# Gate and up with 512 weight columns moving, whole-chunk splits, and two Strassen groups per SwiGLU

## The chip, the cores and the metric

The kernel runs on one core of a Trainium2 chip. The metric is the device time of one execution in microseconds. Three runs of the kernel before gave a median of 753.91 us (753.84 to 754.42). One further execution was recorded by the hardware profiler, and the views quoted below come from that one. The engines are PE (matmul), DVE (vector), ACT (scalar), POOL (GpSimd) and SP, which issues most of the loads.

## The reference, cut to what matters

One decoder layer, x of (1, 256, 1024) in float32, every sublayer between two RMS norms:

```
h = h + 0.5 * rmsnorm(swiglu(rmsnorm(h, g1), w_gate, w_up, w_down), p1)      # FFN1, d_ff = 2816
u = rmsnorm(h, g2)
z, xbc, dt, q, k, v, gates = split(u @ w_in)                                   # the mix stage
h = h + rmsnorm((sig0 * ssd(z, xbc, dt) + sig1 * diff_attn(q, k, v)) @ w_out, p2)
h = h + 0.5 * rmsnorm(swiglu(rmsnorm(h, g3), w_gate, w_up, w_down), p3)      # FFN2
swiglu(x, wg, wu, wd) = (silu(x @ wg) * (x @ wu)) @ wd
```

## The kernel before, in words

There are 256 tokens, two blocks of 128. Every float32 product is made of three products of fp32r parts: an operand is split into hi, an ACT cast (line 167 for weights, line 191 for tokens), and lo, a DVE subtraction (lines 168 and 192), and PE adds hi·hi, lo·hi and hi·lo in PSUM.

Weights come as chunks of 1 MB (128 partitions by 2048 elements), loaded by SP into three raw tiles (`raw`). `split_steps` splits a chunk in two halves of 128x1024, each with its cast and its subtraction into `whi` and `wlo`. `take` hands out the next chunk and first splits on to `AHEAD` = 3 chunks.

The stages follow one another: FFN1 (first products `pn_f`, gate and up `pg_f` and `pup_f`, down `acc_f`), the mix stage (`pn_mx` for v, `pdt` for the time steps with the small weight `wdt`, then `pbc`, `pxs`, `pz`, `pq`, `pgt`, `pws`, `pwd`, and `acc_mx` for w_out), and FFN2 built as FFN1 is.

In an FFN the first 512 of the 2816 gate and up columns go through `norm.products`: here tokens are the stationary operand and 512 weight columns move (`mm_nat`, line 231), the output is natural (a token per partition), and `back` turns it with four transposes per block. The other nine groups of 256 columns go through `mm_w` (lines 215, 216 and 218): weights are stationary, and per 128 rows a matmul of 512 (hi and lo tokens side by side) and one of 256 come out, which puts the output on PE transposed, as the down product needs it. It is evicted by an ACT copy and a DVE addition (lines 219 and 220), multiplied on DVE (line 570) and split (lines 191 and 192). The down product `mm_n` (line 441) keeps the last three chunks (`TAIL`) back, finishes block 0 and then block 1, half after half, so that block 0's norm runs while block 1 is computed.

After each sublayer `post_norm` sums squares (ACT `jp`), takes the root on POOL (`rp`) and updates `h`; then the next norm is made: `sq` on ACT, `r` on POOL, `un` on DVE, eight transposes `pu` on PE, the split into `u`. Up to the end of the first products the order on PE, ACT, DVE and SP is program order (`own_order`); elsewhere a scheduler places the instructions of those engines, with PE held to program order in some stretches. POOL makes small constants (`m3`, `after_m`, `dneg`: masks and distances) and loads gains and small weights by its own queue.

Of the kernel before, what the change touches and what calls it, by code (L numbers as in the profile page):

```python
# [24 lines left out]
P = 128  # L25
T = 256
# [7 lines left out]
K4_BUFS = 29  # L34
K3_BUFS = 3
K2_BUFS = 7
RAW_BUFS = 3
AHEAD = 3
# [5 lines left out]
SSD_US = 1.55  # L44
BREAK, STOP = object(), object()
# [3 lines left out]
def tile_hybrid_layer(ctx: ExitStack, tc: tile.TileContext, x, ffn1_pre_g, ffn1_w_gate, ffn1_w_up,  # L49
# [9 lines left out]

    def k4(shape, name, dt=F32):  # L60
        return sb.tile(shape, dt, tag="k4", name=name, bufs=K4_BUFS)

    def k3(shape, name, dt=F32):
        return sb.tile(shape, dt, tag="k3", name=name, bufs=K3_BUFS)
# [4 lines left out]
    def jk(shape, name):  # L69
        return sb.tile(shape, F32, tag="jk", name=name, bufs=2)  # L70
# [16 lines left out]
    chunks = []  # L87

    def t_chunk(w, k0, c0):
        chunks.append((w[k0:k0 + D, c0:c0 + T].rearrange("(j p) c -> p j c", p=P), [P, KD, T]))  # L90

    def s_chunk(w, k0, c0):
        chunks.append((w[k0:k0 + 512, c0:c0 + 512].rearrange("(j p) c -> p j c", p=P), [P, 4, 512]))

    def n_chunk(w, k0):
        chunks.append((w[k0:k0 + 2 * P, :].rearrange("(j p) c -> p j c", p=P), [P, 2, D]))
# [3 lines left out]

    def ffn_chunks(wg, wu, wd):
        for w in (wg, wu):
            for k0 in (0, 512):
                s_chunk(w[0], k0, 0)
        for j in range(2, FF // T):
            t_chunk(wg[0], 0, j * T)
            t_chunk(wu[0], 0, j * T)
        for j in range(FF // T):
            n_chunk(wd[0], j * T)

    ffn_chunks(ffn1_w_gate, ffn1_w_up, ffn1_w_down)
    for c in range(2):
        for k0 in (0, 512):
            s_chunk(w_in2, k0, V0 + c * 512)
# [9 lines left out]
    for c in range(4):  # L124
        for k0 in (0, 512):
            s_chunk(w_in2, k0, G0 + c * 512)
    for c in range(2):
        for k0 in range(0, 2 * D, 512):
            s_chunk(ssd_w_branch[0], k0, c * 512)
    for c in range(2):  # L130
        for k0 in (0, 512):
            s_chunk(da_w_branch[0], k0, c * 512)
    for c in range(4):
        n_chunk(w_out[0], c * 2 * P)
    ffn_chunks(ffn2_w_gate, ffn2_w_up, ffn2_w_down)

    raws, splits = [], []
    taken = [0]

    def load_to(n):  # L140
        while len(raws) < min(n, len(chunks)):
            i = len(raws)
            src, shape = chunks[i]
            r = sb.tile(shape, F32, tag="raw", name=f"raw{i}", bufs=RAW_BUFS)
            nj = shape[1] // 4 if i == 0 else shape[1] // 2 if i < 4 else shape[1]
            for j in range(0, shape[1], nj):
                nc.sync.dma_start(r[:, j:j + nj, :], src[:, j:j + nj, :])
            raws.append(r)

    def split_steps(ahead=True):  # L150


        i = len(splits)
        load_to(i + 1)
        r, shape = raws[i], chunks[i][1]
        nj = shape[1] // 2
        his, los = [], []
        splits.append((his, los))
        for q in range(2):
            hi = k4([P, nj, shape[2]], f"whi{i}{q}", F32R)  # L160
            lo = k4([P, nj, shape[2]], f"wlo{i}{q}", F32R)
            his.append(hi)
            los.append(lo)
            n = 1 if i == 0 else nj
            for j in range(0, nj, n):
                js = slice(j, j + n)
                nc.scalar.copy(hi[:, js, :], r[:, q * nj + j:q * nj + j + n, :])  # L167
                nc.vector.tensor_sub(lo[:, js, :], r[:, q * nj + j:q * nj + j + n, :], hi[:, js, :].bitcast(F32))  # L168
                yield
        raws[i] = None  # L170
        if ahead:
            load_to(i + 1 + RAW_BUFS)

    def split_to(n):

        while len(splits) < min(n, len(chunks)):
            for _ in split_steps():
                pass

    def take(ahead=AHEAD):  # L180
# [3 lines left out]
        split_to(i + ahead)  # L184
        his, los = splits[i]
        splits[i] = None
        nj = chunks[i][1][1] // 2
        return (lambda j: his[j // nj][:, j % nj, :], lambda j: los[j // nj][:, j % nj, :])
# [17 lines left out]
    def mm_w(dst, name, w, act):  # L206


        (wh, wl), (ah, _, ahl) = w, act
        for m in range(2):  # L210
            acc = pj(f"{name}{m}")
            cs = slice(m * P, (m + 1) * P)
            for j in range(KD):
                if j:
                    nc.tensor.matmul(acc[:, :T], wl(j)[:, cs], ah(j), start=False, stop=False)  # L215
                nc.tensor.matmul(acc, wh(j)[:, cs], ahl(j), start=j == 0, stop=j == KD - 1)  # L216
                if not j:
                    nc.tensor.matmul(acc[:, :T], wl(j)[:, cs], ah(j), start=False, stop=False)
            nc.scalar.copy(dst[:, m, :], acc[:, T:])  # L219
            nc.vector.tensor_tensor(dst[:, m, :], acc[:, :T], dst[:, m, :], ALU.add)  # L220

    def mm_nat(acc, w, act, k0, first, last, late):
# [7 lines left out]
        for i, ((a, b), j) in enumerate(terms):  # L230
            nc.tensor.matmul(acc, a(k0 + j), b(j), start=first and i == 0, stop=last and i == 11)  # L231
# [43 lines left out]
    load_to(RAW_BUFS)  # L275
# [917 lines left out]
```

## Time and profile before

| | us |
|---|---|
| median of three runs | 753.91 |
| span of the profiled execution | 753.1 |
| PE busy in it | 743.7 |
| DVE busy | 521.7 |
| ACT busy | 440.1 |
| POOL busy | 38.2 |
| gate and up of FFN1, from the first `pg_f` to the first `acc_f` | 34.43 to 135.99 |
| down of FFN1 | 135.99 to 196.74 |
| mix stage, from the first `pn_mx` to the first `pn_f` of FFN2 | 196.77 to 562.26 |
| gate and up of FFN2 | 585.67 to 686.88 |

The profiled execution's span is 0.8 us below the median of the runs. A row of the timeline gives the start in the span, the duration, engine, line, operation, the tile written and the tiles read. A row of groups gives, behind the shapes, the count, the busy time in us and the mean duration in ns; behind the second bar stands how long the engine was idle just before, and what released it. Rows of matmuls overlap: what counts is the time from one start to the next.

### The profile page before, as it was taken

The page shows a single profiled execution, that of the slowest core. Times are in us where ns is not written, and L with a number is a line of the kernel's source. Part 1 is how long each engine was busy: PE and PEld are TensorE (multiplying, and loading weights), DVE is VectorE, ACT ScalarE, POOL GpSimd, SP SyncE. Part 2 cuts the span into 40 slices and gives each one's busy share as a digit, 9 for nine tenths or more (in the row PEclk, how much of TensorE's full clock was granted, in tenths as well). Part 3 has the DMA queues.
Part 4 walks back from the last instruction along what each step waited for, and adds up shares of the span by engine and source line. Part 5 has one row for each costly group of instructions (what it writes and reads, how often), then busy time and mean ns, then how long its engine had stood idle before and what let it go on. Part 6 is the DMA issues. An engine that isn't in the chain of part 4 may idle for free.

```text
span 753.1 us, 11054 instructions
## 1 busy us (share of the span) xinstructions
PE 743.7 (99%) x4377; PEld 646.1 (86%) x4377; DVE 521.7 (69%) x792; ACT 440.1 (58%) x737; POOL 38.2 (5%) x72
## 2 busy tenths in 40 slices
PE   8999999999999999999999999999999999999996
PEld 6888888888889999898999788788888888888885
DVE  6686677654577978767778988695684867766612
ACT  7475566643565565858966556784463756565511
POOL 6400000000300000000000000000010000000000
PEclk9999999999999999999999999999999999999999
DMA  8685765587253556565555463467361776555701
GB/s 300 161 265 182 224 224 207 200 286 228 64 166 116 174 163 215 165 210 176 187 168 177 165 219 127 153 224 251 112 225 56 224 224 217 173 173 183 290 1 56
DMA packets 94212, 137.96 MB, mean 183 GB/s; under 512 B 2684, under 2 KB 68304, under 8 KB 94160
## 3 DMA queue, kind: packets, MB, share of 16 engines
q1 hardware_dynamic: 91488, 129.51, 52.5%
q0 software_dynamic: 2368, 7.22, 3.1%
q8 instruction: 34, 0.56, 0.3%
q10 hardware_dynamic: 304, 0.53, 0.2%
q14 instruction: 18, 0.15, 0.1%
HBM read 136.17 MB, written 1.08 MB: 182 GB/s over the span
## 4 chain that ended last, share of the span: by engine, by line
PE 96%; DVE 1%; DMA 1%; POOL 1%; ACT 1%; issue 0%; SPq 0%; DVEq 0%; POOLq 0%
PE acc_f L441 16%; PE pup_f L216 9%; PE pg_f L216 9%; PE pws L231 6%; PE pgt L231 6%; PE pn_f L231 5%; PE pg_f L215 4%; PE pup_f L215 4%; PE acc_mx L441 3%; PE pn_mx L231 3%; PE pwd L231 3%; PE pxs L204 2%; PE pxs L202 2%; PE pxs L201 2%; PE pz L204 2%; PE pz L201 2%
## 5 line engine op out<-in xcount | busy, mean ns | idle before, releaser
L168 DVE TENSOR_TENSOR wlo<-raw,whi 128x1024 fp32r<-128x1024 f32 (+1 forms) x246 | 291.6, 1214 | 56.3 <-ACT whi L167 53.6
L167 ACT CAST whi<-raw 128x1024 fp32r<-128x1024 f32 (+1 forms) x246 | 247.3, 1044 | 59.9 <-PE acc_f L441 21.8
L216 PE MATMUL pg_f<-u_f,whi 128*128 128x512 f32 x288 | 101.2, 396 | 0.0
L216 PE MATMUL pup_f<-u_f,whi 128*128 128x512 f32 x288 | 101.1, 396 | 0.0
L215 PE MATMUL pg_f<-u_f,wlo 128*128 128x256 f32 x252 | 70.5, 280 | 0.0
L215 PE MATMUL pup_f<-u_f,wlo 128*128 128x256 f32 x252 | 70.3, 279 | 0.0
L216 PEld LDWEIGHTS pg_f<-u_f,whi 128*128 128x128 f32 x288 | 52.9, 188 | 9.7
L216 PEld LDWEIGHTS pup_f<-u_f,whi 128*128 128x128 f32 x288 | 52.7, 188 | 9.8
L441 PE MATMUL acc_f<-whi,gh_f 128*128 128x512 f32 x176 | 58.2, 390 | 0.0
L441 PE MATMUL acc_f<-wlo,gh_f 128*128 128x512 f32 x176 | 58.1, 389 | 0.0
L441 PE MATMUL acc_f<-whi,gl_f 128*128 128x512 f32 x176 | 58.1, 389 | 0.0
L215 PEld LDWEIGHTS pg_f<-u_f,wlo 128*128 128x128 f32 x252 | 47.5, 188 | 1.7
L215 PEld LDWEIGHTS pup_f<-u_f,wlo 128*128 128x128 f32 x252 | 47.5, 189 | 1.6
L220 DVE TENSOR_TENSOR su_f<-pup_f,su_f 128x256 f32<-128x256 f32 x36 | 15.2, 423 | 38.7 <-ACT su_f L219 38.7
L441 PEld LDWEIGHTS acc_f<-whi,gl_f 128*128 128x128 f32 x176 | 33.0, 188 | 6.9
L441 PEld LDWEIGHTS acc_f<-wlo,gh_f 128*128 128x128 f32 x176 | 33.0, 188 | 6.8
L441 PEld LDWEIGHTS acc_f<-whi,gh_f 128*128 128x128 f32 x176 | 33.0, 188 | 6.8
L231 PE MATMUL pgt<-whi,u_mx 128*128 128x512 f32 x128 | 34.8, 400 | 0.0
L201 PE MATMUL pz<-u_mx,whi 128*128 128x256 f32 x128 | 32.3, 288 | 0.0
L202 PE MATMUL pz<-u_mx,whi 128*128 128x256 f32 x128 | 31.8, 284 | 0.0
L201 PE MATMUL pxs<-u_mx,whi 128*128 128x256 f32 x128 | 31.7, 285 | 0.0
L202 PE MATMUL pxs<-u_mx,whi 128*128 128x256 f32 x128 | 31.4, 283 | 0.0
(318 smaller groups left out, 1425.9 us busy)
## 6 DMA issues: line engine op xcount, KB each, us to landing
raw<-in_w_in_dram SPq DMA_DIRECT2D x40, 1024.0 KB, 5.4
raw<-in_ffn_w_down_dram SPq DMA_DIRECT2D x22, 1024.0 KB, 5.3
raw<-in_ffn_w_gate_dram SPq DMA_DIRECT2D x20, 1024.0 KB, 5.7
raw<-in_ffn_w_up_dram SPq DMA_DIRECT2D x20, 1024.0 KB, 6.1
raw<-in_ssd_w_branch_dram SPq DMA_DIRECT2D x8, 1024.0 KB, 5.0
acb<-acd POOLq DMA_DIRECT2D x8, 512.0 KB, 4.9
raw<-in_da_w_branch_dram SPq DMA_DIRECT2D x4, 1024.0 KB, 5.1
raw<-in_w_out_dram SPq DMA_DIRECT2D x4, 1024.0 KB, 4.9
```

What stands on the lines that cost most here:

```text
L167: nc.scalar.copy(hi[:, js, :], r[:, q * nj + j:q * nj + j + n, :])
L168: nc.vector.tensor_sub(lo[:, js, :], r[:, q * nj + j:q * nj + j + n, :], hi[:, js, :].bitcast(F32))
L201: nc.tensor.matmul(acc[m], wh(j)[:, cs], ah(k0 + j), start=first and j == ks[0], stop=False)
L202: nc.tensor.matmul(acc[m], wh(j)[:, cs], al(k0 + j), start=False, stop=False)
L204: nc.tensor.matmul(acc[m], wl(j)[:, cs], ah(k0 + j), start=False, stop=last and j == ks[-1])
L215: nc.tensor.matmul(acc[:, :T], wl(j)[:, cs], ah(j), start=False, stop=False)
L216: nc.tensor.matmul(acc, wh(j)[:, cs], ahl(j), start=j == 0, stop=j == KD - 1)
L220: nc.vector.tensor_tensor(dst[:, m, :], acc[:, :T], dst[:, m, :], ALU.add)
L231: nc.tensor.matmul(acc, a(k0 + j), b(j), start=first and i == 0, stop=last and i == 11)
L441: nc.tensor.matmul(acc[b][q], x_[:, ts], w_(kt)[:, halves[q]], start=i == 0 and kt == 0 and x_ is ah and w_ is wh, stop=i == n - 1 and kt ...
```

## The change

Weights are split whole: one ACT cast and one DVE subtraction of 128x2048 per chunk, into rings of three tiles (four inside an FFN). The big work tiles come from a pool of their own per stage (`open_stage`: ffn1, mix, ffn2), which reuses the memory of the one before. `m3`, `after_m`, `dneg` and the v tiles now live in the mix stage's pool; the first that writes them waits until FFN1's stage has been read for the last time.

The nine groups of 256 columns become five groups of natural products, `GROUPS = "hnsns"`. h is 256 gate and 256 up columns side by side, 4 products of 12 matmuls; n is 512 gate and 512 up columns, 8 products; s is the same 512 + 512 columns by Strassen's seven products, where the two halves of the tokens, of the 1024 inputs, and gate against up are the three pairs. s needs four sums of weight tiles (`x1`, and three written over raw tiles), seven weight splits (`q11`, `q3`, `q2`, `q21`, `q1`, `q4`, `q22` in the order of the products), and four forms of the tokens, made once per FFN (`forms`). Every natural output is turned by PE, four slots later (`TURN`): 36 more transposes per FFN.

One call of `product` is one slot: what is due from earlier slots, the 12 matmuls, an eviction that needs this product (`now`), then one step of the weight splits (`pace`). In FFN1 DVE, ACT and SP keep this written order to the end of gate and up, and again in the tail of the down product; in FFN2 the scheduler places DVE, ACT and SP.

```
-K4_BUFS = 29
+MIX_K4 = 20
+FFN_K4 = 11
+TURN = 4
+GROUPS = "hnsns"
...
+        def product(acc, w, f, k0, first, last, go_on=False, now=None, then=None):
+            for d in [d for d in due if d[0] <= slot[0]]:
+                due.remove(d)
+                d[1]()
+            mm_nat(acc, w, f, k0, first, last, "w", go_on)
+            if now:
+                now()
+            pace()
+            if then:
+                then()
+            slot[0] += 1
...
+            one(pa, a11, True, lambda: nc.scalar.copy(pb, pa))
+            one(pd, S["3"], True, lambda: nc.scalar.copy(q7, pd))
+            one(pa, S["2"], False, lambda: nc.vector.tensor_tensor(pd, pa, q7, ALU.add))
+            one(pb, a12, False, None, lambda: act(s0, pb, AF.Silu))
+            one(pa, S["1"], False, lambda: nc.vector.tensor_tensor(q7, pa, q7, ALU.add))
+            one(pd, a22, False, lambda: act(s1, pd, AF.Silu))
+            one(pa, S["4"], False, None, out_)
...
         for i, w in held:
             one(i, w, ((0, (q,)),))
     ready(0)
-    for q in range(2):
-        for i, w in held:
-            if q == 1 and i == n - TAIL:
-                turned()
-            one(i, w, ((1, (q,)),))
-    split_to(taken[0] + AHEAD)
+    while held:
+        if len(held) == 1:
+            turned()
+        one(*held.pop(0), ((1, (0, 1)),))
+    prepare_to(taken[0] + 3)
+    cast_next()
     ready(1)
...
         def unit1(self, engs=(nc.vector, nc.vector)):
             r = rms(1, self.tag)
+            prepare_to(taken[0] + 4)
             self.un = [unit(1, q, r, self.tag, engs[q]) for q in range(2)]
...
-    m3 = const.tile([P, 3, P], F32, name="m3")
+    m3 = stage[1][0].tile([P, 3, P], F32, tag="m3", name="m3", bufs=1)
```

DVE in FFN1's gate and up, before, around the end of one group of 256 columns (`sg` gate, `su` up, `gl` the low part for the down product, numbers are buffers):

```order
L168 TENSOR_TENSOR wlo190_1082<-raw19_935,whi190_1081 128x1024
L220 TENSOR_TENSOR su_f17_976<-pup_f171_1006,su_f17_976 128x256
L168 TENSOR_TENSOR wlo191_1086<-raw19_935,whi191_1085 128x1024
L570 TENSOR_TENSOR sg_f17_926<-su_f17_976,sg_f17_926 128x512
L220 TENSOR_TENSOR sg_f18_1030<-pg_f180_1041,sg_f18_1030 128x256
L192 TENSOR_TENSOR gl_f16_823<-sg_f17_926,gh_f16_822 128x512
```

DVE after, in the second Strassen group of FFN1 (`x1` and the written raw tiles are sums of weights, `wloq2`, `wloq21` and so on the low parts of the products' weights, `pd` and `q7` sums of products):

```order
L300 TENSOR_TENSOR raw19_780<-raw18_762,raw21_822 128x2048
L261 TENSOR_TENSOR wloq2_18_971<-raw18_762,whiq2_18_953 128x2048
L372 TENSOR_TENSOR gl_f14_785<-pt_f129_975,gh_f14_784 128x4x128
L806 TENSOR_TENSOR pd_f14_934<-pa_f14_936,q7_f14_937 128x512
L261 TENSOR_TENSOR wloq21_18_997<-raw21_822,whiq21_18_969 128x2048
L372 TENSOR_TENSOR gl_f14_785<-pt_f130_1001,gh_f14_784 128x4x128
L261 TENSOR_TENSOR wloq1_18_1022<-x1_18_868,whiq1_18_995 128x2048
L808 TENSOR_TENSOR q7_f14_937<-pa_f14_936,q7_f14_937 128x512
L261 TENSOR_TENSOR wloq4_18_1042<-raw19_780,whiq4_18_1020 128x2048
L261 TENSOR_TENSOR wloq22_18_1061<-raw20_804,whiq22_18_1040 128x2048
```

The pieces are twice as long, and the splits of q21 and q4 now stand directly behind additions that read a product.

ACT at the boundary from FFN1 to the mix stage, before (`jp_f10` is block 0's sum of squares after the down product, `jp_f11` block 1's, `sq` those of the next norm, `u` the turned tokens, `v` an eviction of `pn_mx`):

```order
L325 ACTIVATE jp_f110_1781,sp_f11_1780<-acc_f110_1342 128x512
L343 ACTIVATE u0_mx_1698<-pu_mx00_1718,cols_a_109 128x128 x4
L343 ACTIVATE u1_mx_1699<-pu_mx01_1731,cols_a_109 128x128 x4
L167 CAST whi360_1841<-raw36_1634 128x1024
L167 CAST whi361_1845<-raw36_1634 128x1024
L325 ACTIVATE jp_f111_1785,sp_f11_1780<-acc_f111_1343 128x512
L325 ACTIVATE sq_mx10_1795,ss_mx1_1794<-h_72 128x512
```

ACT after, at the same place:

```order
L491 ACTIVATE sq_mx00_1477,ss_mx0_1476<-h_72 128x512
L491 ACTIVATE sq_mx01_1479,ss_mx0_1476<-h_72 128x512
L254 CAST whi35_1496<-raw35_1350 128x2048
L254 CAST whi36_1502<-raw36_1360 128x2048
L491 ACTIVATE jp_f110_1505,sp_f11_1504<-acc_f110_1090 128x512
L491 ACTIVATE jp_f111_1509,sp_f11_1504<-acc_f111_1091 128x512
L491 ACTIVATE sq_mx10_1519,ss_mx1_1518<-h_72 128x512
```

Two casts of 128x2048 stand ahead of both of block 1's sums; before, the first sum stood far ahead and casts of 128x1024 ahead of the second.

POOL before, from the last load of FFN1's start to the end of the constants, which all run early in FFN1:

```order
L635 DMA dsk_1807<-in_ssd_D_dram 16x2
L643 MEMSET m3_1814 128x384
L649 MEMSET after_m_1818 128x128
L645 AFFINE_SELECT m3_1814<-m3_1814 128x128 x2
L650 AFFINE_SELECT after_m_1818<-after_m_1818 128x128
L655 IOTA dneg_1821 128x128
L655 IOTA dneg_1821 128x256
L657 AFFINE_SELECT dneg_1821<-dneg_1821 128x128
L657 AFFINE_SELECT dneg_1821<-dneg_1821 128x256
L660 DMA dtb_1830<-in_ssd_dt_bias_dram 128x32
```

POOL after, from the next norm of block 1 on, at the boundary to the mix stage:

```order
L497 TENSOR_TENSOR r_mx1_1523<-r_mx1_1523,nhalf_97 128x1
...
L547 TENSOR_SCALAR dr_mx_1664<-ident_92,r_mx0_1481 128x128
L948 MEMSET m3_1546 128x384
L954 MEMSET after_m_1550 128x128
L950 AFFINE_SELECT m3_1546<-m3_1546 128x128 x2
L955 AFFINE_SELECT after_m_1550<-after_m_1550 128x128
L960 IOTA dneg_1553 128x128
L960 IOTA dneg_1553 128x256
L962 AFFINE_SELECT dneg_1553<-dneg_1553 128x128
L962 AFFINE_SELECT dneg_1553<-dneg_1553 128x256
L989 DMA wdt_1736<-in_w_in_dram 128x8x32
```

The constants went from the front of the program to this boundary, ahead of the load of `wdt`.

More of the change, by code (lines that the diff above doesn't have):

```diff
@@ L141, in load_to, with load @@
+    def load(n=10 ** 6):
         while len(raws) < min(n, len(chunks)):
             i = len(raws)
[L143 to L158, printed above, removed]
-        for q in range(2):
[L160 to L178, printed above, removed]
+            if sevens and i > sevens[0].c[3] or not (free["sb"] or free["stage"] and not mixing(i)):
+                break
+            parts, nj = chunks[i]
+            raws.append(Raw(f"raw{i}", i, nj))
+            step = nj // 4 if i == 0 else nj // 2 if i < 4 else nj
+            for cols, src in parts:
+                src = src.rearrange("(j p) c -> p j c", p=P)
+                for j in range(0, nj, step):
+                    nc.sync.dma_start(raws[i].t[:, j:j + step, cols], src[:, j:j + step, :])
@@ L183, in take @@
         taken[0] += 1
[L184 to L188, printed above, removed]
+        prepare_to(i + ahead)
+        return pairs.pop(i)
     def split(hi, lo, src):
@@ L204, in mm_t, with mm_nat @@
                 nc.tensor.matmul(acc[m], wl(j)[:, cs], ah(k0 + j), start=False, stop=last and j == ks[-1])
[L206 to L222, printed above, removed]
+    def mm_nat(acc, w, act, k0, first, last, late, go_on=False):
         (wh, wl), (ah, al) = w, act
```

384 lines of the change are left out of this document (321 added, 63 removed).

## The prediction

> **What bounds the kernel now.** I read the page first, for the busy shares and the chain that ended last.
>
> ```profile
> span 753.1 us, 11054 instructions
> PE 743.7 (99%) x4377; PEld 646.1 (86%) x4377; DVE 521.7 (69%) x792; ACT 440.1 (58%) x737; POOL 38.2 (5%) x72
> PEclk9999999999999999999999999999999999999999
> PE 96%; DVE 1%; DMA 1%; POOL 1%; ACT 1%; issue 0%; SPq 0%; DVEq 0%; POOLq 0%
> ```
>
> PE is busy 99% of the span at full granted clock and is 96% of the chain, so a change gains only by taking matmuls away, and loses whatever idle time it opens on PE. I then asked the windows of the stages that change: gate and up of both FFNs, and the boundary from FFN1 to the mix stage.
>
> ```profile
> core 0: us, PE busy (x) PEld busy (x) DVE busy (x) ACT busy (x) POOL busy (x), PEclk, DMA share, GB/s
> 34.43:135.99 101.56, 101.56 (x583) 88.26 (x581) 70.18 (x95) 60.87 (x93) 0.53 (x1) 1.00 0.65 213
> 190.00:215.00 25.00, 25.00 (x121) 20.84 (x120) 16.18 (x35) 16.05 (x38) 4.84 (x8) 1.00 0.19 53
> 585.67:686.88 101.21, 101.21 (x581) 88.08 (x580) 69.68 (x93) 60.08 (x92) 0.63 (x1) 1.00 0.66 213
> ```
>
> PE never stands still in them; DVE has 30% to spare in gate and up. DMA is at 0.65 there, and the change loads the same bytes, so I leave DMA out. The groups of instructions give the prices of DVE and ACT (the last two numbers ahead of the second bar are busy us and mean ns):
>
> ```profile
> L168 DVE TENSOR_TENSOR wlo<-raw,whi 128x1024 fp32r<-128x1024 f32 x242 | 288.7, 1221 | 56.3 <-ACT whi L167 53.6 <-PE po L931 1.6 <-PE pws L231 0.6
> L167 ACT CAST whi<-raw 128x1024 fp32r<-128x1024 f32 x242 | 244.9, 1051 | 58.0 <-PE acc_f L441 21.8 <-DMA raw<-in_ffn_w_down_dram 13.4 <-DMA raw<-in_ffn_w_up_dram 13.0
> L192 DVE TENSOR_TENSOR gl_f<-sg_f,gh_f 128x512 fp32r<-128x512 f32 x18 | 12.5, 693 | 10.2 <-ACT gh_f L191 10.2
> L570 DVE TENSOR_TENSOR sg_f<-su_f,sg_f 128x512 f32<-128x512 f32 x18 | 12.4, 689 | 0.3
> L191 ACT CAST gh_f<-sg_f 128x512 fp32r<-128x512 f32 x18 | 11.2, 620 | 25.7 <-DVE sg_f L570 25.7
> ```
>
> From 512 to 1024 columns a DVE operation grows by 1.221 - 0.693 = 0.53 us, an ACT cast by 1.051 - 0.620 = 0.43. No row has 2048 columns; I estimate 1.22 + 2 x 0.53 = 2.28 us on DVE and 1.05 + 2 x 0.43 = 1.91 us on ACT.
>
> **PE's own work.** The timeline of PE gives the chunk of before (each row is the first matmul of a chunk), and the windows of the down products' tile give the long run of 512-wide matmuls:
>
> ```profile
> 46.49 0.39 PE L216 MATMUL pg_f<-u_f,whi 128*128 128x512 f32 x1
> 52.09 0.39 PE L216 MATMUL pup_f<-u_f,whi 128*128 128x512 f32 x1
> 57.68 0.39 PE L216 MATMUL pg_f<-u_f,whi 128*128 128x512 f32 x1
> ...
> 686.90:746.90 60.00, 59.99 (x264) 49.34 (x263) 2.05 (x3) 2.07 (x6) 1.00 0.31 114
> ```
>
> A chunk takes 5.59 us, and one FFN has 18: 100.6 us. Afterwards these columns are 34 products (4 for h, 8 for each n, 7 for each s) of 12 matmuls at 59.99/264 = 0.227 us: 34 x 2.727 = 92.7. The outputs are natural now, so 36 transposes of 128x128 come in per FFN; the boundary rows below have eight from 205.06 to 205.85, 0.099 us each: 3.6. PE's sum falls by 100.6 - 92.7 - 3.6 = 4.3 us per FFN, **8.6 us** in all, if nothing waits.
>
> **DVE in gate and up.** Per FFN it has 32 operations of 128x2048 (2 splits for h, 4 for each n, 7 splits and 4 adds of weights for each s) and about 34 of 128x512 (10 products, 10 splits of transposed outputs, 4 PSUM adds, 10 for the token forms). At full durations that is 32 x 2.28 + 34 x 0.69 = 96.4 us against 96.3 us of PE. Back to back they overlap a little: the row at 210.53 below has three splits in 3.50 us where 3 x 1.22 were 3.66, 0.08 per operation, and this gives 91. So DVE goes from 69% to 95% or more. It fits on average; the order decides whether PE waits.
>
> **FFN1, where DVE keeps program order.** In a Strassen group the weights of the next product are split behind the eviction of the present one. After the third product DVE adds pd = pa + q7 (it must see that product's end), then splits q21; the fourth product needs q21's low part after 4 transposes and its 8 matmuls on the high part. DVE is ready 0.05 + 0.69 + 2.28 + 0.05 = 3.1 us after the third product; PE comes to it after 0.4 + 1.82 = 2.2: 0.9 us lost, 1.3 with a token split ahead of it. After the fifth product the same with q7 and q4 and no transposes: 3.1 - 1.82 = 1.3. The first split behind the seventh product's cast and products adds about 0.5. That is **3.1 us per group, 6.2 us** for two; zero if DVE has run ahead far enough, 8 if each wait is a whole operation longer. A wait in the second group (its first gate tile needs the PSUM buffer of the h group, released by a product that stands behind splits and forms) I take at **1.5**, between 0 and one operation, 2.3. In the down stage the last group's turn adds **0.5** of a late split (0 to 2.3).
>
> **The boundary to the mix stage.** The timeline of before:
>
> ```profile
> 196.77 1.17 PE L231 MATMUL pn_mx<-whi,u_mx 128*128 128x512 f32 x4
> 197.00 0.60 ACT L325 ACTIVATE jp_f<-acc_f 128x512 f32<-128x512 f32 x1 [0.35 <-PE pt_cols_b L640]
> 197.78 0.82 POOL L330 TENSOR_SCALAR rp_f<-sp_f 128x1 f32<-128x1 f32 x1 [4.77 <-ACT jp_f L325]
> 200.13 0.63 ACT L325 ACTIVATE sq_mx<-h 128x512 f32<-128x512 f32 x1 [2.45 <-DVE h L420]
> 202.60 1.02 DVE L373 TENSOR_SCALAR un_mx<-h,r_mx 128x512 f32<-128x512 f32 x2 [1.89 <-POOL r_mx L331]
> 203.29 1.00 POOL L682 DMA_DIRECT2D wdt<-in_w_in_dram  x1
> 205.06 1.03 PE L340 MATMUL pu_mx<-ident,un_mx 128*128 128x128 f32 x8
> 205.85 1.17 PE L231 MATMUL pn_mx<-whi,u_mx 128*128 128x512 f32 x4
> 209.46 2.94 ACT L167 CAST whi<-raw 128x1024 fp32r<-128x1024 f32 x3
> 210.53 3.50 DVE L168 TENSOR_TENSOR wlo<-raw,whi 128x1024 fp32r<-128x1024 f32 x3 [1.49 <-ACT whi L167]
> 217.61 0.40 ACT L191 CAST wdt_h<-wdt 128x256 fp32r<-128x256 f32 x1
> 219.80 0.28 PE L692 MATMUL pdt<-u_mx,wdt_h 128*32 128x256 f32 x1
> ```
>
> Block 1's normalized tokens are ready at 202.60 + 1.02 = 203.62 and PE turns them at 205.06: 1.4 us of slack. The change puts two casts of 1.91 us ahead of block 1's jp on ACT and a split of 2.28 ahead of un on DVE, and both halves of block 1 finish together, so that a second jp (0.60) comes behind the last matmul. If the casts start only there, pu is 3.8 + 0.6 - 1.4 = 3.0 late; if they are done before, 0. I take **1.7**, since their raw tiles land during the last down chunks. POOL's constants move from early FFN1 to this place, because they now live in the mix stage's memory, which opens when chunk 34's split has been read last:
>
> ```profile
> 20.16 0.44 POOL L643 MEMSET m<- 128x384 f32 x1
> 20.67 2.28 POOL L645 TENSOR_SCALAR_AFFINE_SELECT m<-m 128x128 f32<-128x128 f32 x2
> 22.91 0.29 POOL L650 TENSOR_SCALAR_AFFINE_SELECT after_m<-after_m 128x128 f32<-128x128 f32 x1
> 24.26 0.57 POOL L660 DMA_DIRECT2D dtb<-in_ssd_dt_bias_dram  x1
> ...
> DMA to landing us min/median/max: 3.2/3.2/3.2
> ```
>
> They take 24.26 - 20.16 = 4.1 us, and the wdt load is queued on POOL behind them. The stage opens two products (5.45 us) ahead of pdt. In the same memory lies v, so the third pair of products waits for its eviction: **0.9** (0 to 2). wdt is then ready 4.1 + 3.2 + 0.4 = 7.7 us after the opening and pdt due after 5.45 + 0.9 = 6.35: **1.4** (0 to 3). Boundary: 1.7 + 0.9 + 1.4 = 4.0.
>
> The same select of 128x128 took 1.14 us twice and 0.29 once in these rows. The Trainium skill (SBUF — State Buffer, "SBUF: two separate sides") says that a VectorE operation with two SBUF inputs and a GpSimd operation that reads SBUF lock each other out for a whole instruction. The trace agrees in kind with its 1.14 against 0.29. By that rule the selects would wait for splits of 2.28 instead of 1.22, the wdt term would be about 3 us instead of 1.4, and the sum below 8.7 instead of 7.1; its full price is rival C.
>
> **The mix stage and the ends.** The chain of waits has one place in the mix stage where a split was on the path:
>
> ```profile
> 303.59 1.28 ACT L238
> 304.88 1.06 ACT whi L167
> 305.97 1.23 DVE wlo L168
> ```
>
> A whole chunk is cast and split there in 1.91 + 2.28 = 4.2 us instead of 1.06 + 1.23 = 2.3: 1.9 us more. DVE and ACT carry the same number of elements, in pieces that keep other steps waiting longer. I take **2.0**, between 0 (the scheduler finds room) and 4.5 (two more such places). At the mix stage's end and FFN2's beginning the boundary recurs without constants, **1.0** (0 to 3). The tail:
>
> ```profile
> 746.50 0.39 PE L441 MATMUL acc_f<-wlo,gh_f 128*128 128x512 f32 x1
> 746.92 0.60 ACT L325 ACTIVATE jp_f<-acc_f 128x512 f32<-128x512 f32 x1 [3.39 <-PE acc_f L441]
> 749.69 0.34 ACTq L528 DMA_DIRECT2D out_dram<-h  x1
> ```
>
> One jp stands behind the last matmul; with both halves ending together there are two, **+0.5** (0 to 0.6). FFN2's gate and up is placed by the scheduler, which puts the splits of q21 ahead of the pd add; there I take no stall.
>
> **Sum.** -8.6 + 6.2 + 1.5 + 0.5 + 4.0 + 2.0 + 1.0 + 0.5 = +7.1 us on the span of 753.1. The median of the runs, 753.9, stands 0.8 above the span, so I expect 753.9 + 7.1 = **761.0**. What this kernel's measurement can tell from no change is about 0.2%, 1.5 us.
>
> **The rivals.**
> A, the cover holds: DVE runs ahead in the n groups, where it has 4 splits and 4 small operations for 8 products (4 x 2.28 + 4 x 0.69 = 11.9 us of work in 8 x 2.73 = 21.8), and the Strassen groups live on that lead. Then the stalls of FFN1 go, and half of the boundary and mix with them: -8.6 + 2.0 + 1.0 + 0.5 + 0.5 = -4.6, **749.3**; with no stall at all 745.3. It decides if two prepared products of lead, which the three buffers of split weights allow, are worth the 3.1 us that DVE needs after an eviction. For it: DVE's sum does fit. Against it: in FFN1 the code writes the split behind the eviction that waits for the product, and DVE cannot pass it. 0.20, of which 0.16 faster and 0.04 same.
> B, DVE and ACT become the bound: the sum at full durations, 96.4 of 96.3, leaves nothing, so FFN2 stalls as FFN1 does (6.2 + 1.5 = 7.7) and the mix term is at 4.5: 761.0 + 7.7 + 2.5 = **771**. For it: the raw durations; against: operations overlap when back to back, as in the row at 210.53. 0.13.
> C, POOL's constants: if the two selects on m and two of the others are each held for a split, the chain of 4.1 grows by 4 x 2.28 less the 2 x 1.14 + 2 x 0.29 that they took, some 6 us, and pdt waits about 7: 761.0 + 6 = **767**. For it: the 1.14 beside the 0.29; against: half of what DVE does there reads PSUM. 0.05. The rule on the shared port pair named above would do this. The page's clock was full throughout; the Trainium skill (TensorE: Matmul & The Clock Gate, "Part 1: The HAM clock gate") says that an idle window of about 3.4 us halves it, which no run here shows, and which only a wait like C's would reach.
> That the change doesn't do what it says: the matmuls are counted in the built program, so I give it nothing.
>
> **How the numbers follow.** Forecast 0.62, with its own range 756 to 770 (the bounds of the terms do not all fall on one side); A 0.20, B 0.13, C 0.05. Slower by over 0.2% holds the forecast, B and C: 0.80; faster 0.16; same 0.04. From 750 to 772 the range leaves out A's better half and B's worse half, under 0.2 together.
>
> **What would show it.** Right: PE's 512-wide matmuls still 0.227 us apart; DVE over 90% busy in FFN1's gate and up; gaps of 0.9 to 1.3 us on PE ahead of low-part matmuls in the s groups, released by DVE's splits, and few in FFN2; pdt released by wdt. Wrong: no such gaps (then A), or gaps in FFN2 as many as in FFN1 (then B), or 128x2048 operations far from 2.28 and 1.91 us.

## The result and the profile after

The changed kernel took 771.8 us (770.06 to 772.43, 4 runs) against 754.16 before: ratio 1.023, interval 1.0216 to 1.0245, so 17.6 us slower. The forecast was 761.0, 7.1 us slower. The direction was right, the size not: ten of the seventeen microseconds have to be found.

The page of the changed kernel, for the rows that opened the prediction:

```profile
span 768.3 us, 10269 instructions
PE 747.3 (97%) x4113; PEld 628.5 (82%) x4113; DVE 563.8 (73%) x666; ACT 430.8 (56%) x583; POOL 41.7 (5%) x72
PE 81%; DVE 7%; ACT 6%; issue 3%; POOL 1%; DMA 1%; SPq 0%; DVEq 0%; ACTq 0%; POOLq 0%
```

Two things stand in it. PE is only 81% of the chain, so other engines hold it up, as forecast. But PE is also busy 747.3 us where it was busy 743.7, although it has 264 matmuls fewer: the matmuls themselves take longer, which the prediction did not forecast. The windows of FFN1's gate and up, of the boundary and of FFN2's gate and up (columns as before) show both:

```profile
33.72:139.22 105.50, 100.34 (x445) 79.13 (x443) 88.18 (x67) 56.52 (x52) 0.55 (x1) 1.00 0.51 173
202.67:231.15 28.48, 23.98 (x109) 18.85 (x107) 17.57 (x30) 16.24 (x31) 9.99 (x21) 1.00 0.45 121
601.67:699.72 98.05, 98.05 (x443) 79.87 (x442) 91.55 (x65) 60.11 (x53) 0.63 (x1) 1.00 0.58 205
```

In FFN1 PE stands still for 105.50 - 100.34 = 5.2 us. In FFN2 it never does, and yet needs 98.05 us for the same products. DVE is at 91.55 of 98.05 us there, 93%. The waits of PE, with total, number and longest:

```profile
PE pu_mx L506 <- DVE un_mx L542: 2.7, 1, 2.7
PE pd_f L395 <- DVE wloq L261: 2.3, 2, 1.1
PE pb_f L395 <- DVE wloq L261: 1.8, 2, 0.9
...
PE pu_f L506 <- DVE un_f L542: 1.1, 1, 1.1
PE pdt L999 <- ACT wdt_h L371: 1.0, 1, 1.0
PE pg_f L395 <- DVE sg_f L768: 0.9, 1, 0.9
PE pn_mx L395 <- ACT v L981: 0.8, 1, 0.8
```

All but the row of `pu_f`, which stands at the beginning of FFN2, are the forecast waits, each at its place. And these are the estimated prices (2.28 and 1.91 us) in the rows of groups:

```profile
L261 DVE TENSOR_TENSOR wlo<-raw,whi 128x2048 fp32r<-128x2048 f32 x98 | 224.1, 2290 | 94.0 <-ACT whi L254 93.4
L254 ACT CAST whi<-raw 128x2048 fp32r<-128x2048 f32 x98 | 185.7, 1905 | 127.9 <-PE acc_f L610 39.5 <-PE pxs L382 21.7 <-PE pwd L395 14.2
```

What remains is the spacing of PE's matmuls. The chain of waits shows it in long runs without a wait. First the down products of FFN1 and the first products of the mix stage before:

```profile
136.15 55.77 PE acc_f L441 x246
...
197.00 8.22 PE pn_mx L231 x36
```

Then the down products after:

```profile
148.60 50.55 PE acc_f L610 x218
```

55.77/246 is 0.2267 us per matmul, 50.55/218 is 0.2319. The clock was granted in full in both. The matmuls have the same shapes; what differs is where their operands lie. The allocation of the built programs gives the start byte of each tile in its partition. I took the time from each 512-wide matmul's start to the next one's out of the trace (those under 0.262 us, so without waits), and grouped them by the start, modulo 256 bytes, of the moving tile and of the stationary tile of the next matmul:

```
kernel            moving  stationary  intervals  mean us
before              160        160        1382    0.2276
after                32        160        1645    0.2327   (rings of split weights)
after               160        160         418    0.2285   (tiles in the stages' pools)
```

In the changed kernel the weights come from rings that happen to start at byte 32 of a 256-byte line, and 3 of these 1645 intervals are at 0.226 or 0.227 us, where 1139 of the 1382 before are. In all rows weights move over tokens, but for 72 of the 1382 before, where tokens move over weights.

### The profile page after: what moved, and what is told of

It is laid out like the page before. It is cut to its first block, busy times and chain, and to the rows that moved or that the text cites. A ratio compares the mean times of both kernels' runs of the same rounds, so it can differ in the third digit from the quotient of the medians.

```text
span 768.3 us, 10269 instructions
## 1 busy us (share of the span) xinstructions
PE 747.3 (97%) x4113; PEld 628.5 (82%) x4113; DVE 563.8 (73%) x666; ACT 430.8 (56%) x583; POOL 41.7 (5%) x72
## 4 chain that ended last, share of the span: by engine, by line
PE 81%; DVE 7%; ACT 6%; issue 3%; POOL 1%; DMA 1%; SPq 0%; DVEq 0%; ACTq 0%; POOLq 0%
PE acc_f L610 15%; PE pu_f L395 6%; PE pg_f L395 5%; PE pws L395 5%; PE pgt L395 4%; PE pa_f L395 4%; PE pn_f L395 3%; ACT whi L254 3%; PE pwd L395 3%; DVE wlo L261 3%; PE pd_f L395 3%; PE pxs L382 2%; PE pxs L384 2%; PE pxs L381 2%; PE pz L382 2%
## 5 line engine op out<-in xcount | busy, mean ns | idle before, releaser
L261 DVE TENSOR_TENSOR wlo<-raw,whi 128x2048 fp32r<-128x2048 f32 (+2 forms) x116 | 243.5, 2109 | 96.1 <-ACT whi L254 94.0
L254 ACT CAST whi<-raw 128x2048 fp32r<-128x2048 f32 (+2 forms) x116 | 202.1, 1759 | 131.8 <-PE acc_f L610 39.5
L254 ACT CAST whiq<-raw 128x2048 fp32r<-128x2048 f32 x24 | 45.9, 1911 | 28.4 <-PE pu_f L395 11.8
L261 DVE TENSOR_TENSOR wloq<-raw,whiq 128x2048 fp32r<-128x2048 f32 x24 | 54.7, 2285 | 6.4 <-ACT whiq L254 6.4
L395 PE MATMUL pg_f<-whi,u_f 128*128 128x512 f32 x128 | 32.9, 399 | 0.9 <-DVE sg_f L768 0.9
L395 PE MATMUL pu_f<-whi,u_f 128*128 128x512 f32 x128 | 32.2, 394 | 0.0
L395 PEld LDWEIGHTS pg_f<-whi,u_f 128*128 128x128 f32 x128 | 23.5, 188 | 6.5 <-DVE sg_f L768 1.4
L395 PEld LDWEIGHTS pu_f<-whi,u_f 128*128 128x128 f32 x128 | 24.0, 188 | 5.5
L395 PE MATMUL pn_f<-whi,u_f 128*128 128x512 f32 x96 | 25.1, 395 | 0.0
L381 PEld LDWEIGHTS pz<-u_mx,whi 128*128 128x128 f32 x128 | 24.1, 189 | 0.5 <-issue 0.5
```

What stands on the lines that cost most here:

```text
L254: i = nc.scalar.copy(got["hi"](j, step), src()[:, j:j + step, :])
L261: nc.vector.tensor_sub(got["lo"](j, step), src()[:, j:j + step, :], got["hi"](j, step).bitcast(F32))
L381: nc.tensor.matmul(acc[m], wh(j)[:, cs], ah(k0 + j), start=first and j == ks[0], stop=False)
```

## The experiments

All times are medians beside runs of the kernel before on the same chip, whose medians lie between 753.82 and 754.24. The changed kernel itself was timed once, beside 754.16, so a difference from its 771.8 holds to a few tenths of a microsecond.

**The rings moved by 128 bytes.**

```
-        return sb.tile([P, n], F32, tag=f"tiny{n}", name=name, bufs=10)
+        return sb.tile([P, n], F32, tag=f"tiny{n}", name=name, bufs=14 if n in (1, 6) else 10)
```

> The changed kernel with one edit: four more buffers of a one-column tile, so that the rings of split weights start 128 bytes further on in a partition (byte 160 of a 256-byte line instead of 32), and four more of a six-column tile, so that the tiles of the stages stay where they were modulo 256. Nothing computed changes. In the trace of the changed kernel 512-wide matmuls follow each other every 0.2328 us where the weights move from the rings (1648 intervals, nearly none at 0.227) and every 0.2286 where they move from the stages' tiles (419 intervals, mostly 0.227); before, all were at 0.2276 and started at byte 160. Theory, the start address of the moving weights sets the spacing: some 2200 matmuls return to 0.227, 10 to 13 us are gained, about 760 us. Rival, the spacing comes with the 128x2048 casts and subtractions that read and write SBUF beside PE: spacing stays at 0.2325 and the time at 771 within 1.5 us.

Measured: 765.73 us, ratio 1.0148 (1.0132 to 1.0165), 6.1 us less than the changed kernel. The 2062 intervals are now all 160 to 160 and have a mean of 0.2278. The down products, from its chain:

```profile
147.75 49.44 PE acc_f L610 x218
```

49.44/218 = 0.2268, the old spacing, with the same casts and subtractions beside it. The rival falls. The gain is smaller than 10 us, because FFN1's gate and up, where PE waits for DVE, gave back only 0.8 us (105.50 to 104.69); FFN2's gave 1.7. A second reason is given with the next experiment.

**The kernel before with its work tiles moved by 128 bytes.**

```
-        return sb.tile([P, n], F32, tag=f"tiny{n}", name=name, bufs=10)
+        return sb.tile([P, n], F32, tag=f"tiny{n}", name=name, bufs=14 if n == 2 else 10)
...
+    pad = sb.tile([P, 32], F32, tag="pad", name="pad", bufs=1)
+    nc.gpsimd.memset(pad, 0.0)
     raw_u = [k4([P, 4, 2, P], f"raw_u{q}", F32R) for q in range(2)]
```

> The kernel before with one edit: a tile of 128 bytes ahead of the large work tiles, so that split weights and the tokens of the down products start at byte 32 of a 256-byte line instead of 160 (u, the normalized tokens, stays at 160; a POOL memset of the pad is added). Theory, the moving operand's own start sets the spacing: all 512-wide matmuls with weights moving (about 1380) go from 0.227 to 0.232, 7 to 8 us slower, about 762; the down products are among them. Second form of it, the difference between moving and stationary start matters: only the products with u stationary (first products, gates, the attention branch, about 580) slow down, 3 us, about 757, and the down products stay at 0.227. Rival, whole-chunk splits cause the spacing: no change, 754.

Measured: 755.48 us, ratio 1.0017 (1.0007 to 1.0027), 1.2 us slower. Where split weights move over u (32 against 160, 443 intervals) the mean is 0.2325; where both lie in the moved tiles (32 and 32, 867 intervals) it is 0.2275. Its chain, the same two runs as above:

```profile
136.38 55.78 PE acc_f L441 x246
...
197.24 8.38 PE pn_mx L231 x36
```

The down products did not change (55.78 against 55.77), the first products of the mix stage did (8.38 against 8.22). So for weights that move over tokens it is not the start of the moving tile but its difference from the stationary one: the second form holds for them.

Its price came out at 1.2 us and not 3, because the same difference made PE quicker in the mix stage, where tokens move over weights. Measured from start to start in the same way, the 256-wide matmuls there, with tokens at byte 160, went from 0.1198 us to 0.1187 when the weights went from byte 160 to 32: 1.4 us less over 1301 intervals, against 443 x 5.2 ns = 2.3 us more for the weights that move. In the FFNs, where 512 and 256 wide alternate with tokens moving, some intervals got longer and others shorter, 0.3 us more in all; 2.3 - 1.4 + 0.3 is the 1.2 us. The changed kernel has the quicker 256-wide spacing too (0.1188, tokens at 160 over weights at 32), and the rings moved by 128 bytes lose it again (0.1198, 1292 intervals, 1.3 us). So unequal start bytes are not slow in themselves; it matters which operand moves.

**The rings moved by 64 bytes.** The same edit with other numbers of buffers.

```
+        return sb.tile([P, n], F32, tag=f"tiny{n}", name=name, bufs={1: 12, 6: 16}.get(n, 10))
```

> The changed kernel with the rings moved by 64 bytes instead of 128 (byte 96 of a 256-byte line, the stationary tokens at 160, the stages' tiles at 160 as before). So far a difference of 0 modulo 256 between moving and stationary start gave 0.2275 and one of 128 gave 0.2325. First form, only a half line of difference is slow: 0.2275 and 765 to 766 us, as with 128 bytes. Second form, any difference is slow: 0.232 and 771. Third form, the cost grows with the difference: between them, 0.229 to 0.231 and about 768.

Measured: 771.32 us, ratio 1.0226 (1.0211 to 1.0241); 1639 intervals at 96 against 160 have a mean of 0.2333. For weights that move over tokens the second form holds: of the differences tried, 0 is quick, 64 and 128 are about equally slow. The mix stage's 256-wide matmuls with tokens moving over weights, at 160 against 96, are quickest here, 0.1175 us.

**Block 1's norm ahead of the splits at the end of the down product.**

```
-        prepare_to(taken[0] + 3)
-        cast_next()
         ready(1)
+        prepare_to(taken[0] + 3)
+        cast_next()
...
             r = rms(1, self.tag)
-            prepare_to(taken[0] + 4)
```

> The changed kernel with block 1's norm written ahead of the next weight splits at the end of the down product (ready(1) before prepare_to and cast_next, and no prepare_to between the root and the normalized tokens). Theory of the prediction, the two casts of 128x2048 ahead of block 1's sums on ACT and the split ahead of the normalized tokens on DVE make PE wait for the eight transposes (2.9 us at 211 us in the changed kernel's trace): this wait goes to under 0.5 us, and 2 to 4 us are gained over the two boundaries, about 768. Rival, the weights then become late: the wait only moves to the next products, which need the same casts and splits, and the time stays within 1.5 us of 771.8.

The boundary of the changed kernel, from its timeline:

```profile
202.86 3.75 ACT L254 CAST whi<-raw 128x2048 fp32r<-128x2048 f32 x2
206.46 0.65 ACT L491 ACTIVATE jp_f<-acc_f 128x512 f32<-128x512 f32 x1
210.18 2.29 DVE L261 TENSOR_TENSOR wlo<-raw,whi 128x2048 fp32r<-128x2048 f32 x1
211.17 1.46 POOL L496 TENSOR_SCALAR r_mx<-ss_mx 128x1 f32<-128x1 f32 x1 [2.36 <-ACT sq_mx L491]
213.31 0.88 DVE L542 TENSOR_SCALAR un_mx<-h,r_mx 128x512 f32<-128x512 f32 x2 [0.84 <-POOL r_mx L497]
213.85 1.09 PE L506 MATMUL pu_mx<-ident,un_mx 128*128 128x128 f32 x8 [2.68 <-DVE un_mx L542]
```

The casts run from 202.86, behind the last down product, and jp comes 3.8 us behind it: the case of the prediction's upper bound (3.0 us of wait), not the 1.7 us that I took. A second loss is in POOL's row: 1.46 us where the same operation took 0.30 us before:

```profile
201.62 0.30 POOL L330 TENSOR_SCALAR r_mx<-ss_mx 128x1 f32<-128x1 f32 x1 [2.36 <-ACT sq_mx L325]
```

It ends just behind the DVE split of 210.18 to 212.47. The Trainium skill (SBUF — State Buffer, "SBUF: two separate sides") says that a GpSimd operation that reads SBUF and a VectorE operation with two SBUF inputs hold each other off for a whole instruction; the trace agrees with this 1.46 against 0.30.

Measured with the norm ahead: 770.67 us, ratio 1.022 (1.0204 to 1.0236), 1.1 us less. PE's waits moved, as the rival had it:

```profile
207.73 3.69 ACT L254 CAST whi<-raw 128x2048 fp32r<-128x2048 f32 x2
209.67 1.20 PE L395 MATMUL pn_mx<-whi,u_mx 128*128 128x512 f32 x4 [0.96 <-ACT whi L254]
212.04 1.20 PE L395 MATMUL pn_mx<-wlo,u_mx 128*128 128x512 f32 x4 [1.18 <-DVE wlo L261]
```

**Chunk 35 cast and split during block 1's products, then the norm.**

```
             one(*held.pop(0), ((1, (0, 1)),))
+            if len(held) == TAIL - 1:
+                prepare_to(taken[0] + 3)
-        prepare_to(taken[0] + 3)
-        cast_next()
         ready(1)
+        prepare_to(taken[0] + 4)
...
             r = rms(1, self.tag)
-            prepare_to(taken[0] + 4)
```

> The changed kernel with chunk 35 cast and split while block 1's second held chunk is multiplied (ahead of block 0's turn), block 1's norm then ahead of chunk 36. Writing the norm alone ahead only moved PE's waits from the transposes to chunk 35's cast and split (0.96 and 1.18 us). Theory, the two engines had 5 us of idle time ahead of the boundary that this order uses: PE waits ahead of pn_mx's second group and pu_mx sum to under 1 us instead of 2.9, the 3.4 us at half clock that follow the gap in some executions go too, and the time falls by 3 to 5 us to about 768. Rival, the rings of three have no free tile before block 1 is done (chunks 30 to 32 are held): cast and split start where they did, and the time stays within 1.5 us of 771.

Measured: 767.39 us, ratio 1.0177 (1.0162 to 1.0192), 4.4 us less. The boundary takes 25.56 instead of 28.48 us, and the wait ahead of pu_mx is gone. Of the 4.4 us, 2.9 are this; the rest is in keeping with PE's clock, below.

**The PSUM additions behind the splits.**

```
-            one(pa, S["2"], False, lambda: nc.vector.tensor_tensor(pd, pa, q7, ALU.add))
+            one(pa, S["2"], False, None, lambda: nc.vector.tensor_tensor(pd, pa, q7, ALU.add))
...
-            one(pa, S["1"], False, lambda: nc.vector.tensor_tensor(q7, pa, q7, ALU.add))
+            one(pa, S["1"], False, None, lambda: nc.vector.tensor_tensor(q7, pa, q7, ALU.add))
```

> The changed kernel with the two PSUM additions of a Strassen group (pd after the third product, q7 after the fifth) written behind the weight split of the same slot instead of ahead of it. Theory of the prediction, these additions hold back the split in FFN1 (PE waits of 1.25 and 1.4 us twice each in the trace, 5.3 us): the four waits go to under 0.3 us each and 4 to 5.5 us are gained in FFN1's gate and up, about 767; FFN2, where the scheduler already puts the splits ahead, is unchanged. Rival, DVE has no slack there at all (43 of 50 us busy): the wait moves to the sixth or seventh product, which needs the additions, and at most 1.5 us is gained.

Measured: 768.9 us, ratio 1.0194 (1.0178 to 1.0211), 2.9 us less; FFN1's gate and up 102.68 instead of 105.50. It lies between the two expectations: of the four waits the two ahead of the sixth products go and the two ahead of the fourth shrink from 0.9 to 0.3 us, but two waits of products into pa for their own low parts come, 0.7 us together in the list of waits. Its profile caught something else. PE at the boundary, from its timeline, and windows around it (us, PE, PEld, DVE, ACT, POOL, then the granted clock, 0.50 in the second):

```profile
210.98 1.97 PE L506 MATMUL pu_mx<-ident,un_mx 128*128 128x128 f32 x8 [2.69 <-DVE un_mx L542]
212.60 1.67 PE L395 MATMUL pn_mx<-whi,u_mx 128*128 128x512 f32 x4
```

```profile
208.30:210.28 1.98, 0.00 (x0) 0.00 (x0) 1.29 (x1) 0.00 (x0) 1.90 (x2) 1.00 0.29 100
210.28:213.70 3.42, 2.72 (x11) 2.53 (x12) 1.46 (x5) 1.57 (x7) 3.01 (x6) 0.50 0.83 251
213.70:217.10 3.40, 3.40 (x16) 2.77 (x15) 2.73 (x8) 2.40 (x4) 0.00 (x0) 1.00 0.73 95
```

PE stood still for 2.69 us, from 208.29 on, and 2.0 us into this gap its clock was halved for 3.4 us: eight transposes took 1.97 us instead of 1.09. The Trainium skill (TensorE: Matmul & The Clock Gate, "Part 1: The HAM clock gate") puts this at an idle window of about 3.4 us, in windows that run freely; here a gap of 2.69 us was enough, and only in some executions: the profile of the changed kernel has the same gap at full clock.

The clock records of the thirteen kept traces say when. In each, every halving begins a whole number of 3.413 us after the full clock was first granted (here 60 after 5.48 us). In the 3.413 us that ended there PE had stood still for 2.00 us or more (2.00 here; 2.04 and 2.07 are the next). In no such stretch at full clock that was not followed by a halving had it stood still for more than 1.77 us. In the changed kernel's trace the border of two stretches, at 212.08, cut the gap into 0.91 and 1.77 us. So it is chance, by where the gap falls, whether it costs more than itself.

What it costs is seen at the boundary: 29.74 to 30.07 us in the profiles of this kernel and of two others with the half clock there (the rings moved by 64 bytes, FFN1 left to the scheduler), against 28.48, so 1.3 to 1.6 us. Three of the changed kernel's four runs, 771.25 to 772.43, have a mean clock of 0.996 against 0.998 in the profiled one of 770.06, which is in keeping with it. With chunk 35 cast early the gap is gone, and the four runs' clocks are 0.998 and 0.999.

**FFN1's gate and up left to the scheduler.**

```
         norm.products(ws or [take(1) for _ in range(4)], evict, at, **kw)
+        if tag == "f1":
+            free_order()
+            own_order(PE)
```

> The changed kernel with DVE, ACT and SP of FFN1's gate and up left to the scheduler, PE held to its order, as in FFN2 already; the scheduler then puts the splits of q21, q1 and q4 ahead of the pd addition. Theory of the prediction, the program order of DVE makes FFN1's waits: FFN1's gate and up falls from 105.5 us to FFN2's 98 to 99.5, 6 to 7 us gained, about 765. Rival, FFN2 is quicker for other reasons (its loads are ahead, no setup work): 103 us or more in FFN1, 769 or more.

Measured: 764.45 us, ratio 1.0135 (1.0119 to 1.0151), 7.3 us less. FFN1's gate and up:

```profile
33.78:132.33 98.55, 98.55 (x445) 80.00 (x443) 92.72 (x67) 60.20 (x54) 0.55 (x1) 1.00 0.59 209
```

PE never stands still in it, with DVE busy 92.72 us of 98.55. The written order of DVE, ACT and SP together made the waits, not DVE's load; which part of it DVE's own order has, this edit does not tell.

**No Strassen group.**

```
-GROUPS = "hnsns"
+GROUPS = "hnnnn"
```

> The changed kernel with GROUPS hnnnn: no Strassen group, the token forms not made, 36 products instead of 34 per FFN. Theory, PE's count rules where nothing waits: FFN2's gate and up gets 2 x 2.79 = 5.6 us longer (98.05 to 103.6), FFN1's gets 5.6 longer and loses its four waits and the late splits of 6.2 us (105.5 to 105): 777 in all. Rival, the sums, forms and extra splits of the Strassen groups hold back more than that, and FFN1 falls below 103: 774 or less.

Measured: 777.35 us, ratio 1.0313 (1.0296 to 1.033). FFN2's gate and up takes 103.67 us, FFN1's 104.28. PE's count ruled; in FFN1 the Strassen groups' waits ate more than two products saved (105.50 with them). That the total agrees is in part luck: this execution had the clock halved for 3.41 us at the beginning of FFN2, which took 2.5 us longer than in the changed kernel.

**wdt's load ahead of the constants.**

```
     norm = made[0]
+    wdt = k2([P, KD, H_SSD], "wdt")
+    nc.gpsimd.dma_start(wdt, w_in2[:, DT0:DT0 + H_SSD].rearrange("(j p) c -> p j c", p=P))
     open_stage("mix", MIX_K4)
...
-    wdt = k2([P, KD, H_SSD], "wdt")
-    nc.gpsimd.dma_start(wdt, w_in2[:, DT0:DT0 + H_SSD].rearrange("(j p) c -> p j c", p=P))
```

> The changed kernel with the load of wdt issued on POOL ahead of the constants, nothing else. Theory of the prediction, wdt is late because it is queued behind the constants, which wait for the stage: PE's wait of 1.0 us ahead of pdt goes, and the boundary's 28.5 us fall to 27.5. Rival, the wait is for ACT, which casts wdt behind other work: it stays at 0.5 us or more.

Measured in a single execution: the wait ahead of pdt is gone from the list of PE's waits. The boundary was 29.18 us and the run 772.1, since this execution had the half clock at 215.9 us; so the shorter boundary is not shown by time. Against the 29.74 to 30.07 us of the three others with the half clock there it is 0.6 to 0.9 us shorter.

**The four edits together** (rings by 128 bytes, FFN1 to the scheduler, chunk 35 early, wdt ahead).

> The changed kernel with four edits together: the rings moved by 128 bytes (6.0 us gained alone), FFN1's gate and up left to the scheduler, chunk 35 cast early and the norm first, and the load of wdt issued on POOL ahead of the constants. Theory, the losses are separate and add up: 6 + 6 to 7 + 3 to 5 + 1 us, about 755, between 752 and 758, with PE's 512-wide spacing at 0.2275 and no wait of PE over 1 us in FFN1 and at the boundary. Rival, one cause lies under all (DVE's load of over 90% in gate and up), so that one wait takes the place of another: 760 or more.

Measured: 751.36 us, ratio 0.9966 to the kernel before (0.9953 to 0.9979), 20.4 us less than the changed kernel and 2.5 less than the kernel before. FFN1's gate and up and the boundary:

```profile
32.92:129.74 96.82, 96.82 (x445) 79.84 (x443) 92.58 (x67) 60.29 (x54) 0.55 (x1) 1.00 0.59 212
191.44:215.63 24.19, 23.36 (x108) 19.01 (x107) 14.73 (x30) 13.59 (x28) 8.90 (x21) 1.00 0.56 144
```

The gains add up a little beyond their sum (6.1 + 7.3 + 4.4 and 1 us for wdt), so the causes are separate, and where PE no longer waits the quicker spacing counts in full: in FFN1's gate and up it gave 98.55 - 96.82 = 1.7 us, where it had given 0.8.

**The four edits without Strassen groups.**

> The kernel with the four edits together (751.4 us) and GROUPS hnnnn, so without Strassen groups. Theory, with nothing waiting in gate and up, PE's count alone decides: two products of 2.73 us more per FFN, 5.5 us in FFN1 (96.8 to 102.3) and 5.5 in FFN2 (96.4 to 101.8), 762. Rival, the Strassen groups still cost PE hidden waits: under 759.

Measured: 764.93 us, ratio 1.0136 (1.0119 to 1.0152). Gate and up take 102.28 and 101.88 us, as expected; 2.4 us more than expected are at the beginning of FFN2, where PE waited 2.3 us and the clock was halved for 3.4 us from 577.3 on. Strassen's groups are worth 2 x 5.5 us of PE where nothing waits.

## Why the prediction was right and wrong

By stages, in the profiled executions (span 753.1 to 768.3, +15.2):

| term | forecast | measured | with the rings moved |
|---|---|---|---|
| FFN1, gate and up and down | +3.9 | +6.6 | +4.6 |
| boundary to the mix stage, `pn_mx` to `pdt` | +4.0 | +5.5 | +5.4 |
| mix stage, `pdt` to `acc_mx` | +2.0 | +2.2 | +1.7 |
| `acc_mx` to FFN2's gate and up | +1.0 | +2.5 | +2.4 |
| FFN2, gate and up and down | -4.3 | -1.0 | -3.9 |
| tail, and the start | +0.5 | -0.5 | -0.5 |
| sum | +7.1 | +15.2 | +9.7 |

The step that failed is the first one of PE's work: "34 products ... of 12 matmuls at 59.99/264 = 0.227 us". I carried the spacing over because the matmul's shape did not change. It was 0.2327 for the 1645 intervals with weights from the rings, because these tiles started at another byte of a 256-byte line than the tokens. FFN2, where PE did not wait, shows the term almost alone: gate and up took 98.05 us where the sum has 92.7 + 3.6 = 96.3, and 96.38 with the rings moved; the down products, for which the sum has no change, took 61.80 instead of 59.62, and 60.55 with the rings moved. Moving the rings back to the tokens' byte took 5.5 us off the span and 6.1 off the median. The list of what would show the prediction right did begin with this spacing, but no rival was made of its failing.

The mechanism of FFN1's waits was right, and nearly their size: the fourth and sixth products of a Strassen group took 4.05 and 4.18 us where FFN2's took 2.87 and 2.79, so 1.2 and 1.4 us lost (forecast 0.9 to 1.3, and 1.3), and the order of FFN1 cost 105.50 - 98.55 = 7.0 us in all (forecast 6.2 + 1.5). The second group's first gate tile cost 0.9 (forecast 1.5). With the rings moved, FFN1 and FFN2 are within 0.7 us of the forecast. One sign did not come: DVE was busy 88.18 of 105.50 us in FFN1's gate and up, 84% and not over 90.

The boundary's mechanism was right too, but the casts' term was mis-sized: they ran at the place of the upper bound, 2.7 us of wait instead of 1.7, part of it (1.46 - 0.30 us) by POOL's operation held off by a DVE split. v cost 0.8 (forecast 0.9), wdt 1.0 (1.4). Rival C fell: POOL's constants were quick where they are now,

```profile
224.06 0.55 POOL L950 TENSOR_SCALAR_AFFINE_SELECT m<-m 128x128 f32<-128x128 f32 x2
...
226.04 0.97 POOL L989 DMA_DIRECT2D wdt<-in_w_in_dram  x1
```

0.55 us for the two selects that took 2.28 before. But DVE stood still beside them:

```profile
225.02 2.16 DVE L561 SCALAR_TENSOR_TENSOR us_mx<-pu_mx,cols_a,rbs_mx 128x128 f32<-128x128 f32 x8 [4.19 <-ACT rbs_mx L556]
```

It was idle for the 4.19 us ahead of this row, from 220.83 on. The rule of the Trainium skill on the shared port (SBUF — State Buffer, "SBUF: two separate sides") was weighed at the wrong operation: it had no occasion there, and what agrees with it is the small operation of the norm's root above.

The mix stage's +2.2 meets its forecast of 2.0 by luck. That term was for whole-chunk casts and splits on the path, and between `pdt` and `acc_mx` PE's list has no wait for a weight's cast or split; PE was idle there for 1.4 us instead of 0.5 and busy for 319.6 instead of 318.3.

The rest of the 17.6 us is between the span and the median: the profiled execution of the changed kernel was its quickest, and the half clock, which I had tied to rival C alone, came with the 2.7 us gap ahead of pu_mx in most runs, by their mean clocks. The prediction's "which no run here shows" was wrong as well: its own trace has the half clock at the end, from 751.38 us, after the last matmul.

Rival A (no waits) was wrong for this kernel and is what the four edits make of it; rival B was wrong: FFN2 did not wait once with DVE at 93%.

The next beginning, from acc_mx to FFN2, cost 2.5 us instead of 1.0. Of it 1.1 is PE's wait for the normalized tokens (`pu_f`), with POOL's small operation held off once more, beside a DVE split of 582.46 to 584.75:

```profile
583.76 1.16 POOL L496 TENSOR_SCALAR r_f<-ss_f 128x1 f32<-128x1 f32 x1 [4.32 <-ACT sq_f L491]
```

The rest was not taken apart. Why start bytes change PE's rate, why the other way round where tokens move in 256-wide runs, and what differences besides 64 and 128 do, stays open.

## What to carry to other kernels

A matmul's spacing belongs to its operands' places as well as to its shape: when a change lays tiles out anew, compare the start bytes of moving and stationary tiles modulo 256 before taking over the old figure, measure rather than assume which way a difference goes, and read the spacing in long runs of the chain first, since a PE that is "busy" may only be slow. An engine that is 93% busy need not stall its neighbour; an instruction that waits ahead of others in its program order will, so ask of each eviction what is queued behind it. And a gap on PE of over two microseconds can cost some 1.5 us more by a half clock that sets in during or behind it, in some executions only.

## What the runs showed of the hardware

- 512-wide fp32r matmuls with weights moving over tokens followed each other every 0.2273 to 0.2286 us (0.2267 in undisturbed runs) where moving and stationary tile started at the same byte modulo 256, and every 0.2325 to 0.2333 us at differences of 64 and 128.
- In runs of 256-wide ones with tokens moving over weights it was the other way round: every 0.1198 us at the same byte, 0.1187 to 0.1189 at a difference of 128 and 0.1175 at 64.
- The granted clock was halved for 3.41 us at the end of every stretch of 3.413 us at full clock, counted from the first full clock, in which PE had been idle for 2.00 us or more, and never after 1.77 us or less (thirteen traces); so a gap of 2.69 us halved it and one of 2.68 us, cut in two by such a border, did not.
- A one-column POOL operation took 1.46 us instead of 0.30 beside a DVE subtraction of 128x2048.
- A DVE subtraction of 128x2048 took 2.29 us and an ACT cast 1.905, as the growth from 512 to 1024 columns had given (2.28 and 1.91).
